# Delta-rule merges on all four 64x64 quarters of the array, with half of the diagonal blocks placed by ScalarE

## The chip, the cores and the metric

The kernel runs on one NeuronCore of a Trainium2 chip. The metric is device time in microseconds, the median of several executions. A profile is one more execution, recorded by the hardware profiler. Five engines run side by side: TensorE (PE; its weight loads are listed as PEld), VectorE (DVE), ScalarE (ACT), GpSimd (POOL) and SyncE (SP), which here only issues DMAs. Each works through its own queue in the order in which the program put the instructions there.

## The reference, cut to what matters

The layer has two branches. Branch A is a chunked gated delta rule over 8 heads and two directions, with chunks of 64 tokens. For every head and chunk the reference solves a unit lower-triangular system:

```python
a_mat = jnp.where(strict, jnp.einsum('nbhid,nbhjd->nbhij', kc * bc[..., None], kc) * decay, 0.0)
eye = jnp.eye(CHUNK, dtype=a_mat.dtype)
t_mat = lax.linalg.triangular_solve(eye + a_mat, jnp.broadcast_to(eye, a_mat.shape),
                                    left_side=True, lower=True)
```

so `t_mat` is the inverse of a 64x64 unit triangular matrix. The rest (projections with a combined `w_in`, a short convolution, the scan over chunks, differential attention in branch B, gates and the output projection) surrounds it. The sequence has 1024 latent and 256 context tokens, 1280 in all, which the kernel holds as `NT` = 10 pieces of 128 tokens; each piece has two chunks of 64. Everything is fp32; the projections split fp32 into two fp32r parts.

## The kernel before, in words

**Inverting the blocks.** `gdn_prep(h)` prepares one head. A tile `X` holds, for both directions and the 10 pieces, a 128x128 matrix. The inverse is built from blocks that double in size. The 32x32 diagonal blocks are inverted by substitution on VectorE (lines 1156 to 1161) and come back through DRAM as `R`, with `Rt` its transposed copy. Below, B(0) to B(3) are the four groups of 32 partitions, and `lo` and `hi` the two halves of 64.

Then come four groups of small matmuls, each put into TensorE's queue in one go through `mms`:

- `pz`, 32x32: 40 products, on four of the sixteen 32x32 places of the array (line 1176). VectorE writes `Z` = -pz.
- `p2` and `p3`, 32x32: 60 products on six places (line 1186). `p2` holds corner blocks for `X`; `p3` holds the corners of the 64x64 blocks for a tile `t64`, which has one 64x64 block for each of the 20 chunks. The products into `p3` share the rows of the array with a product into `p2` (B(0) or B(3)) and its columns with another one (B(1) or B(2)), in a PSUM bank of their own. ScalarE copies `p3` into `t64` (lines 1198 and 1199), and `placed` copies four blocks per chunk from `R` and `Rt` into `X` and `t64` (VectorE's line 1250 for `t64`).
- `pz6`, 64x64 (line 1212): for each of the 10 pieces one product that reads partitions `hi` and writes `lo`, and one that reads `lo` and writes `hi`. So the group uses two of the array's four 64x64 quarters, ten products each. The pieces are split over two PSUM banks: pieces 5 to 9 go into the first, pieces 0 to 4 into the second. VectorE writes `Z6` = -pz6.
- `pu6`, 64x64 (line 1222): `t64` times `Z6`, `lo` to `lo` and `hi` to `hi`: the other two quarters alone.

ScalarE copies `pu6` into `X`, scales `X` by `beta` and SyncE stores it, for the scan to load.

In the profile `pz6` and `pu6` appear as `pz` and `pu` with 64*64, since numbers at the end of a name are left out there, and `t64` as `t`. An fp32 product makes two matmul records and two weight loads, so a 64x64 group of 20 products shows 40 records.

**What sets the order.** All parts of the kernel (`gdn_prep` for each head, `placed`, the scans of both directions, the projections, the convolution) are generators that yield one step: engine, a modelled duration, what it depends on, and the function that issues the instructions. A planner (`flow`, `step`) picks the next step by modelled start times and issues it. So the order on each queue is fixed by the modelled durations, not by what happens on the chip. A step's function may issue several instructions; the planner then still counts one step on one engine.

While the heads are prepared, the projection matmuls (`mm`) fill TensorE's queue between the steps of the scan (`chain`, `out`) and of `gdn_prep`. In the scan, each piece goes from TensorE (`chain`) to ScalarE (`vd`, `vn`, lines 1323 and 1327) or VectorE (`r`, `S`) and back to TensorE.

PSUM banks for these steps come from a ring, `banks`; a step that takes a bank waits for the instructions listed with it. The bank of `p3` is listed with the two copies of lines 1198 and 1199, and a later `gram` group of the next head can be the one that takes it.

Of the kernel before, what the change touches and what calls it, by code (L numbers as in the profile page):

```python
# [23 lines left out]
NT = LT // P  # L24
# [10 lines left out]
PE, DVE, ACT, POOL, DMA, ADMA, DV2, PL1 = range(8)  # L35
# [8 lines left out]
class Block:  # L44
# [1040 lines left out]
    def gdn_prep(self, h):  # L1085
        nc, PT, V = self.nc, self.gt_, self.nc.vector
        T = lambda nm, shape, tag=None: self.g1.tile(shape, F32, tag=tag or nm, name=nm)
        G = lambda nm, shape: self.gh[h % 2].tile(shape, F32, tag=nm, name=nm)
        X = G("X", [P, 2, NT, P])
# [24 lines left out]
        for c0 in range(0, NT, 2):  # L1114
# [3 lines left out]
            for j in range(2):  # L1118
                c = c0 + j
# [20 lines left out]
        B = lambda b: slice(32 * b, 32 * b + 32)  # L1140
# [14 lines left out]
        for j in range(31):  # L1155
            n, w = 31 - j, j + 1
# [30 lines left out]
            x for c in range(NT) for x in (  # L1187
                (p2[B(0), c], R[B(0), c], Z[B(0), c]), (p2[B(1), c], Rt[B(1), NT + c], Z[B(1), c]), (p3[B(1), c], Z[B(0), c], R[B(0), c]),
                (p2[B(2), c], R[B(2), c], Z[B(2), c]), (p2[B(3), c], Rt[B(3), NT + c], Z[B(3), c]), (p3[B(2), c], Z[B(3), c], Rt[B(3), NT + c]))), 0.25
# [7 lines left out]
        self.banks.append(tx[:])  # L1197
        t6 = [(yield ACT, 0.43, [t3], lambda: nc.scalar.copy(t64[B(1), :, 0:32], p3[B(1)])),
              (yield ACT, 0.43, [t3], lambda: nc.scalar.copy(t64[B(2), :, 32:64], p3[B(2)]))]
        self.banks.append(t6[-2:])  # L1200
        yield lambda: placed
# [10 lines left out]
        t = yield PE, 1.5, [tx, b], lambda: self.mms(  # L1212
            x for cs, z in zip(halves, pz) for j in range(5) for c in (cs.start + j,) for x in (
                (z[lo, j], X[hi, 0, c, lo], X[hi, 0, c, hi]), (z[hi, j], X[lo, 1, c, hi], X[lo, 1, c, lo]))), 0.5
        tz = []
        for cs, z in zip(halves, pz):
# [23 lines left out]
    def placed(self, X, R, Rt, tt, tz, out):  # L1240
# [3 lines left out]
        tx, t6 = [], []  # L1244
# [3 lines left out]
        for (m, q, f) in ((0, slice(0, 32), R[B(0), 0:NT]), (1, slice(32, 64), R[B(1), 0:NT]), (2, slice(0, 32), Rt[B(2), NT:]),  # L1248
                          (3, slice(32, 64), Rt[B(3), NT:])):
            t6 += [(yield DV2, 0.34, [tt], lambda: V.tensor_copy(t64[B(m), :, q], f))]  # L1250
        yield lambda: tz
# [959 lines left out]
```

## Time and profile before

| | us |
|---|---|
| three runs | 1934.7, 1934.76, 1938.63 |
| their median | 1934.76 |
| the profiled execution, its own time | 1935.46 |
| its span, first to last instruction | 1933.3 |
| TensorE busy | 1896.7 (98%) |
| VectorE busy | 1453.0 (75%) |
| ScalarE busy | 1062.6 (55%) |
| GpSimd busy | 678.8 (35%) |
| first and last start of a 64x64 `pz` record | 603.9 and 1192.1 |

The span is the time from the first to the last instruction; 2.2 us of the profiled execution lie around it. Busy time of TensorE is the union of its matmuls, whose ends are modelled, so a busy share near 100% says that it had always something in flight, and not that it ran at its peak. The granted clock is full in all forty slices of the span. The merges of the eight heads lie between 595 and 1202 us, one head after the other.

### The profile page before, as it was taken

The numbers are of one execution on the slowest core, as the hardware profiler recorded it, in microseconds if no ns is written. First come the engines' busy times: TensorE is split into PE (matmuls) and PEld (weight loads), VectorE is DVE, ScalarE is ACT, GpSimd is POOL, SyncE is SP. The second block draws the span as 40 slices with busy tenths as digits, with TensorE's granted clock in tenths as the row PEclk, the third lists the DMA queues.
The fourth block names the chain that finished last, engine by engine and source line by source line (L and its number), as shares of the span: only waits on it lengthen the run. The fifth ranks groups of instructions, "written<-read, shape, count | busy, mean of one in ns | idle before, by whom it ended". The sixth has DMA issues, their size and how long they took to land.

```text
span 1933.3 us, 37454 instructions
## 1 busy us (share of the span) xinstructions
PE 1896.7 (98%) x13807; PEld 1675.3 (87%) x13807; DVE 1453.0 (75%) x3613; ACT 1062.6 (55%) x2189; POOL 678.8 (35%) x610
## 2 busy tenths in 40 slices
PE   6999999999999999999999999999999999999999
PEld 4878888899999998888888888888997888888887
DVE  4687998957887887867865865338996979995677
ACT  4543444426233563677576645439885868884222
POOL 3200000005441342343333332336766667672203
PEclk9999999999999999999999999999999999999999
DMA  9144535575545567667785565666336474226542
GB/s 335 58 137 96 138 95 138 123 190 179 165 142 183 183 191 228 216 204 232 213 292 175 195 199 150 212 231 224 132 124 210 158 238 151 93 88 213 186 157 87
DMA packets 383038, 336.39 MB, mean 174 GB/s; under 512 B 142609, under 2 KB 323443, under 8 KB 381831
## 3 DMA queue, kind: packets, MB, share of 16 engines
q1 hardware_dynamic: 382855, 333.99, 55.0%
q8 instruction: 109, 1.79, 0.4%
q14 instruction: 74, 0.61, 0.1%
HBM read 222.14 MB, written 111.79 MB: 173 GB/s over the span
## 4 chain that ended last, share of the span: by engine, by line
PE 84%; DVE 6%; DMA 4%; ACT 3%; issue 2%; SPq 1%; POOL 1%; DVEq 0%; ACTq 0%; POOLq 0%
PE mm L56 43%; PE s L56 7%; PE v L56 5%; PE chain L56 5%; PE mb L56 5%; PE ma L56 4%; PE x L56 3%; PE t L63 3%; PE out L56 3%; PE gram L56 1%; DVE S L1567 1%; DVE ac L595 1%; PE pz L56 1%; PE tr L63 1%; SPq L265 1%
## 5 line engine op out<-in xcount | busy, mean ns | idle before, releaser
L56 PE MATMUL mm<-hs,wh 128*128 128x512 f32 (+1 forms) x2048 | 648.7, 390 | 1.5 <-DVE hs L408 1.4
L56 PEld LDWEIGHTS mm<-hs,wh 128*128 128x128 f32 x2048 | 371.3, 189 | 58.7 <-DVE hs L408 2.0
L56 PE MATMUL mm<-hs,wl 128*128 128x512 f32 (+1 forms) x1024 | 397.8, 388 | 1.0 <-POOL wl L886 1.0
L56 PE MATMUL mm<-wh,hs 128*128 128x256 f32 (+1 forms) x1792 | 332.7, 286 | 0.2 <-ACT sq L978 0.2
L56 PEld LDWEIGHTS mm<-wh,hs 128*128 128x128 f32 x1792 | 281.0, 191 | 0.7 <-ACT sq L978 0.4
L1567 DVE TENSOR_SCALAR_CACHE_REDUCE S<-s,rsq 128x512 f32<-128x512 f32 (+1 forms) x384 | 239.8, 655 | 26.9 <-DMA vl<-vd 12.0
L56 PE MATMUL mm<-wl,hs 128*128 128x256 f32 (+1 forms) x896 | 256.0, 286 | 0.0
L1604 POOL TENSOR_TENSOR S<-S 128x1280 f32<-128x1280 f32 x64 | 188.9, 2955 | 92.2 <-ACT S L1597 90.9
L56 PEld LDWEIGHTS mm<-hs,wl 128*128 128x128 f32 x1024 | 194.0, 189 | 29.8 <-POOL wl L886 1.4
L1580 ACT ACTIVATE S<-S,mn 128x1280 f32<-128x1280 f32 x128 | 175.2, 1372 | 51.3 <-DVE mn L1579 50.9
L56 PEld LDWEIGHTS mm<-wl,hs 128*128 128x128 f32 x896 | 171.4, 191 | 0.1
L595 DVE SCALAR_TENSOR_TENSOR ac<-xc,convT,ac 128x1284 f32<-128x1284 f32 (+1 forms) x96 | 138.8, 1448 | 11.2 <-ACT ac L593 10.6
L56 PE MATMUL s<-kk,qh 128*128 128x512 f32 (+1 forms) x384 | 142.7, 372 | 1.9 <-DVE S L1567 1.7
L56 PE MATMUL s<-kk,ql 128*128 128x512 f32 (+1 forms) x384 | 132.9, 358 | 0.0
L1641 DVE TENSOR_TENSOR al<-t,ah 128x512 fp32r<-128x512 f32 (+1 forms) x192 | 107.0, 595 | 7.6 <-ACT ah L1636 6.3
L580 POOL MEMSET xc<- 128x2 f32 (+1 forms) x64 | 3.6, 100 | 298.5 <-ACT sq L629 113.1
L1160 DVE TENSOR_TENSOR ts<-ts,tmp 80x31 f32<-80x31 f32 (+15 forms) x248 | 94.1, 380 | 6.0
L1323 ACT ACTIVATE vd<-chain,edk 128x128 f32<-128x128 f32 x144 | 52.2, 370 | 77.8 <-PE chain L56 71.9
L56 PE MATMUL ma<-y,wh 128*128 128x512 f32 x256 | 93.0, 410 | 1.7 <-DVE g L1814 1.7
L1158 DVE TENSOR_TENSOR tmp<-ab,ts 80x31 f32<-80x31 f32 (+15 forms) x248 | 89.2, 360 | 6.6 <-DMA ab<-da 1.3
L1636 ACT CAST ah<-t 128x512 fp32r<-128x512 f32 (+1 forms) x192 | 87.9, 521 | 9.0 <-PE t L63 8.3
L56 PE MATMUL v<-al,vh 128*128 128x256 f32 x320 | 90.9, 284 | 0.7 <-DVE al L1641 0.6
(296 smaller groups left out, 4315.7 us busy)
## 6 DMA issues: line engine op xcount, KB each, us to landing
wr<-in_w_in_dram SPq DMA_DIRECT2D x48, 512.0 KB, 5.7
hx<-in_w_in_dram SPq DMA_DIRECT2D x64, 256.0 KB, 4.3
x<-xq SPq DMA_DIRECT2D x64, 256.0 KB, 5.1
X<-gcd SPq DMA_DIRECT2D x8, 1280.0 KB, 7.1
kd<-col SPq DMA_DIRECT2D x40, 256.0 KB, 2.2
xq<-X SPq DMA_DIRECT2D x16, 640.0 KB, 8.9
kk<-kd SPq DMA_DIRECT2D x16, 640.0 KB, 6.4
kq<-gkq SPq DMA_DIRECT2D x8, 1152.0 KB
```

The source lines that it names most:

```text
L56: self.nc.tensor.matmul(out, lhsT, rhs, start=start, stop=stop)
L63: self.nc.tensor.transpose(out, src, self.ident[:src.shape[0], :src.shape[0]])
L265: return DMA, us, list(deps), lambda: nc.sync.dma_start(dst, src)
L595: t = yield DV2, 1.21e-3 * wd, [t], lambda: nc.vector.scalar_tensor_tensor(ac[:, :wd], xc[:, j:j + wd], self.convw(j, x["ct"]), ac[:, :wd] ...
L1158: t = yield DV2, n * w / 960.0 + 0.08, [t if j else self.later(t, 2.5), t1], lambda: V.tensor_tensor(tv, ab[:, j + 1:, j:j + 1].to_broadca ...
L1160: t = yield DV2, n * w / 960.0 + 0.08, [t, t1], lambda: V.tensor_tensor(ts[:, j + 1:, :w], ts[:, j + 1:, :w], tv, ALU.subtract)
L1323: td = yield ACT, 0.251, [t], lambda: nc.scalar.activation(vd, pc[:, 1], AF.Copy, scale=self.edk[:, c, g:g + 1])
L1567: e = yield DVE, 0.675 if m == 512 else 0.408, [e, self.sfree[c].get(n - 4 + c)], lambda: self.nc.vector.tensor_scalar(x["S"][c][:, o:o + ...
L1580: x["x"].append((yield ACT, 1.36, [e], lambda: nc.scalar.activation(S, S, AF.Exp, bias=x["mn"][:, c:c + 1], scale=-1.0, accum_out=w["l0"][ ...
L1604: e = yield POOL, 2.9, [e], lambda: self.nc.gpsimd.tensor_tensor(S0, S0, S1, ALU.add)
L1636: e = yield ACT, 0.48 if nb == 4 else 0.27, [t, y["old", k]], lambda: self.nc.scalar.copy(y["ah", k][:, :, q], pv)
L1641: t = yield DVE, 0.603 if k < 2 else 0.322, [e, y["old", k]], lambda: self.nc.vector.tensor_tensor(y["al", k][:, :, q], pv, y["ah", k][:, ...
```

## The change

Four places change.

1. In the `p3` products, pieces 5 to 9 write the two corners to other partitions: B(3) in place of B(1), and B(0) in place of B(2).
2. The copies of `p3` into `t64` and the copies of `R`/`Rt` into `t64` are cut into pieces 0 to 4 and pieces 5 to 9. For the last five pieces the two 64x64 blocks of a piece stand in swapped halves of the partitions. The corners take four ScalarE copies of 32x5x32 in place of two of 32x10x32. Of the four VectorE copies in `placed`, each is cut to five pieces, and the same step now also issues a ScalarE copy for the other five. The planner's modelled durations and engines are as they were.
3. `pz6`: for pieces 5 to 9 the product from `hi` writes `hi` and the one from `lo` writes `lo`. The order is now piece 0, piece 5, piece 1, piece 6 and so on, so four products in a row use the four quarters.
4. `pu6`: pieces 5 to 9 read the swapped blocks of `t64` and `Z6`, so their products run from `hi` to `lo` and from `lo` to `hi`, in the same mixed order. The results stand where they stood.

```diff
         t = t3 = yield PE, 1.3, [tz, b], lambda: self.mms(
             x for c in range(NT) for x in (
...
+                (p2[B(0), c], R[B(0), c], Z[B(0), c]), (p2[B(1), c], Rt[B(1), NT + c], Z[B(1), c]),
+                (p3[B(1 if c < 5 else 3), c], Z[B(0), c], R[B(0), c]),
+                (p2[B(2), c], R[B(2), c], Z[B(2), c]), (p2[B(3), c], Rt[B(3), NT + c], Z[B(3), c]),
+                (p3[B(2 if c < 5 else 0), c], Z[B(3), c], Rt[B(3), NT + c]))), 0.25
...
-        t6 = [(yield ACT, 0.43, [t3], lambda: nc.scalar.copy(t64[B(1), :, 0:32], p3[B(1)])),
-              (yield ACT, 0.43, [t3], lambda: nc.scalar.copy(t64[B(2), :, 32:64], p3[B(2)]))]
-        self.banks.append(t6[-2:])
+        fs, ls = slice(0, 5), slice(5, 10)
+        corner = lambda m, n, q: (nc.scalar.copy(t64[B(m), fs, q:q + 32], p3[B(m), fs]), nc.scalar.copy(t64[B(n), ls, q:q + 32], p3[B(n), ls]))
+        t6 = [(yield ACT, 0.43, [t3], lambda: corner(1, 3, 0)),
+              (yield ACT, 0.43, [t3], lambda: corner(2, 0, 32))]
+        self.banks.append(t6[:])
...
         t = yield PE, 1.5, [tx, b], lambda: self.mms(
-            x for cs, z in zip(halves, pz) for j in range(5) for c in (cs.start + j,) for x in (
-                (z[lo, j], X[hi, 0, c, lo], X[hi, 0, c, hi]), (z[hi, j], X[lo, 1, c, hi], X[lo, 1, c, lo]))), 0.5
+            x for c in range(5) for f, e in ((c, lo), (c + 5, hi)) for g in (hi if e is lo else lo,) for z in (pz[f < 5],) for x in (
+                (z[e, c], X[hi, 0, f, lo], X[hi, 0, f, hi]), (z[g, c], X[lo, 1, f, hi], X[lo, 1, f, lo]))), 0.5
...
         t = yield PE, 1.5, [tz, t6, b], lambda: self.mms(
-            x for cs, u in zip(halves, pu) for j in range(5) for c in (cs.start + j,) for x in (
-                (u[lo, j], t64[lo, c], Z6[lo, c]), (u[hi, j], t64[hi, c], Z6[hi, c]))), 0.5
+            x for c in range(5) for f, e in ((c, lo), (c + 5, hi)) for g in (hi if e is lo else lo,) for u in (pu[f < 5],) for x in (
+                (u[lo, c], t64[e, f], Z6[e, f]), (u[hi, c], t64[g, f], Z6[g, f]))), 0.5
...
-            t6 += [(yield DV2, 0.34, [tt], lambda: V.tensor_copy(t64[B(m), :, q], f))]
+            t6 += [(yield DV2, 0.34, [tt], lambda: (V.tensor_copy(t64[B(m), :5, q], f[:, :5]), nc.scalar.copy(t64[B(m ^ 2), 5:, q], f[:, 5:])))]
```

The queues of GpSimd and SyncE hold the same instructions in the same order in both kernels; VectorE's differs only in the size of the copies of `placed` into `t64`. TensorE's and ScalarE's queues differ as follows.

TensorE, at the `pz6` group of head 0, before and with the change (`pz_6191` and `pz_6192` are the banks of pieces 5 to 9 and 0 to 4 before, `pz_6197` and `pz_6198` the same two with the change):

```order
 L56 MATMUL mm<-wl,hs 128x256
 L56 MATMUL mm<-wh,hs 128x256 x2
-L56 MATMUL pz_6191<-X 64x64 x10
-L56 MATMUL pz_6192<-X 64x64 x10
+L56 MATMUL pz_6198<-X 64x64 x2
+L56 MATMUL pz_6197<-X 64x64 x2
```

The two bank rows alternate five times in all with the change: still twenty products, and now in pairs that go to the two banks in turn.

ScalarE around the corner copies of head 5, before (`X<-RR` and `X<-p` place blocks in `X`, `t<-p` are the corner copies, `vd` and `vn` belong to the scan):

```order
L1247 COPY X<-RR 32x10x32 x2
L1196 COPY X<-p_11894 32x10x32
L1323 ACTIVATE vd<-chain,edk 128x128
L1327 COPY vn<-chain 128x128
L1323 ACTIVATE vd<-chain,edk 128x128
L1327 COPY vn<-chain 128x128
L1196 COPY X<-p_11894 32x10x32
L1198 COPY t_3837<-p_11895 32x10x32
L1199 COPY t_3837<-p_11895 32x10x32
```

And the same place with the change:

```order
L1251 COPY X<-RR 32x10x32 x2
L1254 COPY t_3837<-RR 32x5x32
L1198 COPY X<-p_11924 32x10x32
L1254 COPY t_3837<-RR 32x5x32 x2
L1327 ACTIVATE vd<-chain,edk 128x128
L1331 COPY vn<-chain 128x128
L1254 COPY t_3837<-RR 32x5x32
L1327 ACTIVATE vd<-chain,edk 128x128
L1331 COPY vn<-chain 128x128
L1198 COPY X<-p_11924 32x10x32
L1201 COPY t_3837<-p_11925 32x5x32 x4
```

Four new copies (`t<-RR`) stand among the scan's instructions and ahead of the corner copies, and the two corner copies have become four of half the size.

More of the change, by code (lines that the diff above doesn't have):

```diff
@@ L1187, in gdn_prep @@
             x for c in range(NT) for x in (
-                (p2[B(0), c], R[B(0), c], Z[B(0), c]), (p2[B(1), c], Rt[B(1), NT + c], Z[B(1), c]), (p3[B(1), c], Z[B(0), c], R[B(0), c]),
-                (p2[B(2), c], R[B(2), c], Z[B(2), c]), (p2[B(3), c], Rt[B(3), NT + c], Z[B(3), c]), (p3[B(2), c], Z[B(3), c], Rt[B(3), NT + c]))), 0.25
+                (p2[B(0), c], R[B(0), c], Z[B(0), c]), (p2[B(1), c], Rt[B(1), NT + c], Z[B(1), c]),
+                (p3[B(1 if c < 5 else 3), c], Z[B(0), c], R[B(0), c]),
+                (p2[B(2), c], R[B(2), c], Z[B(2), c]), (p2[B(3), c], Rt[B(3), NT + c], Z[B(3), c]),
+                (p3[B(2 if c < 5 else 0), c], Z[B(3), c], Rt[B(3), NT + c]))), 0.25
         tx, e = [], t
```

## The prediction

> **What bounds the kernel now.** I read the page's busy shares first, then the stretch in which the merges lie (590 to 1200 us), and there the chain of waits, the waits of TensorE and the timelines of single groups.
>
> From the page, the table by engine and the chain that ended last:
>
> ```profile
> PE 1896.7 (98%) x13807; PEld 1675.3 (87%) x13807; DVE 1453.0 (75%) x3613; ACT 1062.6 (55%) x2189; POOL 678.8 (35%) x610
> PE 84%; DVE 6%; DMA 4%; ACT 3%; issue 2%; SPq 1%; POOL 1%; DVEq 0%; ACTq 0%; POOLq 0%
> ```
>
> Busy time of each engine in the stretch, then the chain's shares in it and its longest links that are not TensorE's:
>
> ```profile
> 590.00:1200.00 610.00, 605.45 (x5915) 543.90 (x5914) 452.68 (x1275) 361.70 (x1002) 203.42 (x248) 1.00 0.65 206
> by line: PE mm L56 57.2%; PE chain L56 13.6%; PE out L56 7.2%; PE gram L56 3.7%; PE pz L56 2.7%; DMA hx<-tbd 1.8%; PE pu L56 1.7%; issue 1.6%; PE p L56 1.6%; DMA xq<-qk 1.4%; PE tr L63 1.2%; DMA x<-xq 1.0%; PE oT L63 0.8%; DVE fin L999 0.5%
> 624.79 10.85 DMA hx<-tbd
> 752.88 8.75 DMA xq<-qk
> 1060.31 5.95 DMA x<-xq
> ```
>
> TensorE is busy for 605 of 610 us (columns: stretch, then PE, PEld, DVE, ACT, POOL), and its groups make up nine tenths of the chain. All that it waited for there:
>
> ```profile
> PE tr L63 <- DVE fin L1000: 1.0, 1, 1.0
> PE mm L56 <- POOL wl L886: 1.0, 1, 1.0
> PE p L56 <- issue: 0.5, 1, 0.5
> PE chain L56 <- DVE S L1336: 0.5, 1, 0.5
> PE chain L56 <- DVE r L1314: 0.4, 1, 0.4
> PE chain L56 <- DMA x<-xq: 0.4, 1, 0.4
> PE chain L56 <- DVE S L1334: 0.4, 1, 0.4
> PE gram L56 <- ACT t L1199: 0.2, 1, 0.2
> ```
>
> That is 4.4 us. So TensorE's queue sets the time, and a shorter group moves what follows it; the last row also says that in one place the corner copies of `t64` hold TensorE up already.
>
> **The groups on four quarters.** One 64x64 group of head 0 and one 32x32 `pz` group in TensorE's timeline (start, duration, records):
>
> ```profile
> 603.93 1.38 PE L56 MATMUL pz<-X 64*64 64x64 f32 x40
> 605.24 0.39 PE L56 MATMUL mm<-wl,hs 128*128 128x256 f32 x1
> ...
> 595.38 0.89 PE L56 MATMUL pz<-RR,X 32*32 32x32 f32 x80
> 596.20 0.38 PE L56 MATMUL mm<-wh,hs 128*128 128x256 f32 x1
> ```
>
> From the group's first start to the next work it is 605.24 - 603.93 = 1.31 us for 40 records, 20 on each of two quarters. About 0.15 us of that is filling and draining (below, the last record of `p` starts 0.12 us ahead of the next work). So one quarter takes a record every (1.31 - 0.15) / 20 = 0.058 us. With ten records on each of four quarters a group takes 0.15 + 10 x 0.058 = 0.73 us: **0.58 us less**. Bounds: half of 1.31, 0.65, and nothing at all, if quarters that share rows or columns cannot run together.
>
> The row that comes nearest to this is the `p` group, whose products share rows (B(0) and B(3) are read twice) and columns, with different PSUM banks for the latter, just as the new order has it:
>
> ```profile
> 856.15 0.22 PE L56 MATMUL p<-Z,RR 32*32 32x32 f32 x2
> 856.16 0.21 PE L56 MATMUL p<-RR,Z 32*32 32x32 f32 x1
> 856.17 0.22 PE L56 MATMUL p<-Z,RR 32*32 32x32 f32 x2
> 856.18 0.21 PE L56 MATMUL p<-RR,Z 32*32 32x32 f32 x1
> ...
> 857.18 0.19 PE L56 MATMUL p<-RR,Z 32*32 32x32 f32 x1
> 857.30 0.50 PE L56 MATMUL mm<-hs,wh 128*128 128x512 f32 x1
> ```
>
> 120 records take 1.15 us. In the 32x32 `pz` group each place has 20 records in 0.82 us, about 0.035 us a record without filling. If a strip of rows did one product at a time, the 40 records of B(0) in `p` would need 1.4 us; they took 1.15, the whole group being paced at about 9 ns a record. So products that share rows do overlap. At 9 ns, 40 records need 0.36 us, less than 0.73, so issue doesn't bound the new groups. I take 0.58.
>
> Two rules of the Trainium skill speak against this. Its page "TensorE: Matmul & The Clock Gate", section "Part 3: Packing small matmuls — row/col tiling", says that a weight load overlaps running matmuls only where the row group differs; by that the two quarters of a row half would take turns (rival 2). The trace so far disagrees, by the 1.15 us of `p`. The same page of the skill, section "Back-to-back issue gap", states a floor of about 25 ns for small matmuls; by an estimate from it 40 records would need 1.0 us and the sum below would come to some -1 us. The trace disagrees here too, with 80 records in 0.82 us.
>
> Sixteen groups (8 heads, `pz` and `pu`): 16 x 0.58 = **9.3 us** of TensorE's time.
>
> **How much of it reaches the end.** The groups of heads 0 and 1 (four, 2.3 us) lie before or between the chain's DMA links at 624.79 and 752.88, where TensorE is not what sets the time: the transposes of `fin` already wait 1.0 us, and by the time of the second link the lead is gone. The other twelve follow, 7.0 us. The link at 1060.31 is a load of what a head stored before, so it moves with the work ahead of it. I take 0.2 us off for small waits: **6.8 us** arrive. Bounds: 9.3 if the DMA links move too, and 2.2 if the link at 1060.31 holds as well, since the eight groups of heads 2 to 5 (4.6 us) lie ahead of it.
>
> **ScalarE's added work.** Durations of copies in the stretch, by shape (count, busy us, mean ns):
>
> ```profile
> L885 ACT CAST wh<-hx 128x512 fp32r<-128x512 f32 x52 | 31.1, 616 | 5.4 <-DMA hx<-in_w_in_dram 5.1
> L1327 ACT COPY vn<-chain 128x128 f32<-128x128 f32 x103 | 27.1, 266 | 7.3 <-PE chain L56 7.3
> L1247 ACT COPY X<-RR 32x320 f32<-32x320 f32 x32 | 14.5, 454 | 1.0 <-DMA RR<-db 0.5
> L1198 ACT COPY t<-p 32x320 f32<-32x320 f32 x8 | 3.3, 417 | 0.2
> ```
>
> From SBUF, 320 columns take 454 ns and 512 take 616, so 0.84 ns a column and about 320 ns for 160. From PSUM, 128 take 266 and 320 take 417: 0.79 a column, about 291 ns for 160. A head adds four copies of 0.32 and turns two of 0.417 into four of 0.291: 1.28 + 1.16 - 0.83 = 1.61 us, and 12.9 us over eight heads. ScalarE is idle for 610 - 362 = 248 us of the stretch, mostly for TensorE:
>
> ```profile
> ACT zo L1039 <- PE mm L56: 57.1, 30, 5.3
> ACT vd L1323 <- PE chain L56: 55.9, 39, 4.2
> ```
>
> so most of the added work falls into its waits. It costs where TensorE waits for what is queued behind it: the bank of `p3`, which `gram` takes, and `vd` and `vn` of the scan. ScalarE and TensorE at head 3, and ScalarE at head 5 with TensorE's `gram` there:
>
> ```profile
> 859.13 0.42 ACT L1198 COPY t<-p 32x320 f32<-32x320 f32 x1
> 859.56 0.42 ACT L1199 COPY t<-p 32x320 f32<-32x320 f32 x1
> ...
> 860.03 0.71 PE L56 MATMUL gram<-kq 128*128 128x128 f32 x4 [0.17 <-ACT t L1199]
> ...
> 1021.47 0.42 ACT L1196 COPY X<-p 32x320 f32<-32x320 f32 x1 [0.47 <-PE p L56]
> ...
> 1022.62 0.27 ACT L1327 COPY vn<-chain 128x128 f32<-128x128 f32 x1
> 1023.79 0.42 ACT L1199 COPY t<-p 32x320 f32<-32x320 f32 x1
> ...
> 1024.63 0.38 PE L56 MATMUL gram<-kq 128*128 128x128 f32 x2
> ```
>
> At head 3 `gram` starts 0.05 us after the second corner copy, so the corners' extra 1.16 - 0.83 = 0.33 us is lost in full. At head 5 the first new copy fits into the idle 0.47 us; the other three (0.96) and the corners (0.33) push the release of the bank from 1023.79 + 0.42 = 1024.21 by 1.29 us, against 0.42 - 0.05 = 0.37 us of room before `gram`: 0.9 us lost. The other heads have one to four copies ahead of a `vd` or `vn`; I put them at 0.3 us each, one copy's length, the rest being idle time: 6 x 0.3 = 1.8. Together **3.0 us**. Bounds: the two places that the rows show, 1.2, and all of 12.9.
>
> **VectorE.** Its four copies a head are cut in half:
>
> ```profile
> L1250 DVE COPY t<-RR x32: 307/318/814, 602.9 to 1190.2; 32x320 f32<-32x320 f32 x32
> ```
>
> At most 4 x 0.16 = 0.64 us a head. VectorE is idle for 157 us of the stretch and these copies are followed by the substitution of a later head; I count nothing, and up to 1 us as a bound. The `p3` products only change place: 0. The evacuations of `pz6` and `pu6` find both banks complete at the end of the group, where before one was ready halfway; that end is now as early as the old half: 0.
>
> **The sum.** -6.8 + 3.0 - 0.2 (VectorE) = -4.0 us. From the profiled execution's own 1935.46 (span 1933.3 and 2.2 around it) that gives 1931.5; it lies 0.7 above the median of 1934.76, so the median should come to **1930.8**.
>
> **Rivals.**
>
> 1. *ScalarE's copies are hidden and the DMA links move with TensorE.* For it: 248 us of idle ScalarE. Against it: the two `gram` places. Between -5.5 and -9.3; at its end 1925.5.
> 2. *Quarters that share rows take turns.* The groups gain nothing and ScalarE's 3.0 us stay: 1937.8. Against it: the `p` group.
> 3. *Quarters that share PSUM partitions half overlap*, since two products then write the same partitions at once. A group gains half, 0.29 us, 16 x 0.29 = 4.6, of which by the same share (6.8 of 9.3) 3.4 arrive; with +3.0 and -0.2 about 1934.2. Against it: B(1) and B(2) in `p`, which two products write.
> 4. *Slower: ScalarE becomes what the scan waits for.* The planner does not count the new copies, so they stand among `vd` and `vn`, and each may delay the recurrence that two directions share. If all 12.9 us reach TensorE, the sum is +6.1: 1940.9. It decides from the point where more than 10.7 us of the 12.9 (6.8 + 3.9) are exposed. For it: the order at head 5. Against it: 113 us in which `zo` and `vd` wait for TensorE.
>
> **How the numbers follow.** Chances: the forecast 0.64, rival 1 0.15, rival 2 0.08, rival 3 0.05, rival 4 0.08. A difference of 0.2% is 3.9 us, about what a measurement of this kernel can tell from none, and the forecast sits on that edge: somewhat over half of its chance (0.35) lies beyond it. Faster: 0.35 + 0.15 = 0.50. Within 0.2%: 0.29 of the forecast, 0.05 of rival 3, and 0.06 of rival 2, whose +3.0 stays mostly under the edge: 0.40. Slower: 0.02 of rival 2 and 0.08 of rival 4: 0.10. The range takes in most of rival 1 and a part of rival 2: 1926.5 to 1936.5.
>
> **What the profile of the changed kernel would show.** Right: 64x64 groups that last about 0.73 us from first start to the next work, ScalarE busy about 13 us more, VectorE 2 to 4 us less, TensorE's waits for `gram` and `chain` behind ScalarE 2 to 3 us longer, and a lead at TensorE that grows between 760 and 1200 us and is constant after. Wrong in the first term: groups still at 1.3 us (rival 2) or at 1.0 (rival 3). Wrong in the second: a lead of 9 us at 1200, or one lost at a DMA link. Wrong in the third: TensorE's waits for ScalarE near zero, or above 10 us.

## The result and the profile after

| | before | with the change |
|---|---|---|
| median of the runs, us | 1936.36 (22 runs) | 1933.22 (22 runs) |
| lowest to highest | 1932.28 to 1938.63 | 1930.07 to 1937.47 |
| ratio to before, 95% interval | | 0.9986 (0.998 to 0.9992) |
| profiled execution, its span | 1935.46, 1933.3 | 1933.29, 1931.2 |

The change is **2.7 us faster** by the ratio (1936.36 x 0.0014; by the interval 1.5 to 3.9). That is a gain that the runs can tell from nothing, but it lies within 0.2%. The forecast was -4.0 us, 1930.8. Of the 2.4 us by which 1933.22 misses it, 1.6 come from the first three runs of before, whose median of 1934.76 was low, and the rest from the sum (the two medians lie 3.1 us apart, the ratio says 2.7). The prediction gave 0.50 to a gain beyond 0.2% and 0.40 to one within it; it was the second.

The page of the changed kernel, its table by engine; then, by engine, the stretch in which the merges lie (columns as in the prediction):

```profile
PE 1890.5 (98%) x13807; PEld 1665.9 (86%) x13807; DVE 1450.8 (75%) x3613; ACT 1075.3 (56%) x2237; POOL 678.1 (35%) x610
```

```profile
590.00:1200.00 610.00, 600.94 (x5920) 535.98 (x5919) 451.73 (x1278) 375.74 (x1057) 202.69 (x248) 1.00 0.65 206
```

ScalarE has 14.0 us more in the stretch (361.70 before), VectorE only 0.95 less, TensorE 4.5 less. The span fell by 2.1 only. TensorE's waits in the stretch, the longer ones (what waited, for what: us in total, times, longest):

```profile
PE tr L63 <- DVE fin L1000: 1.2, 1, 1.2
...
PE gram L56 <- ACT t L1201: 1.0, 2, 0.5
PE pu L56 <- DVE Z L1221: 0.9, 1, 0.9
PE chain L56 <- DVE S L1340: 0.8, 2, 0.5
...
PE chain L56 <- DMA sk<-gkq: 0.6, 1, 0.6
PE chain L56 <- DMA vv<-gv: 0.5, 1, 0.5
PE chain L56 <- DVE r L1318: 0.5, 1, 0.5
PE tr L63 <- DVE Z L1221: 0.4, 1, 0.4
...
PE chain L56 <- ACT vn L1331: 0.4, 1, 0.4
```

All rows together add up to 8.5 us, against 4.4 before. New are the waits for `Z` (VectorE), for `vn` (ScalarE) and for `sk` and `vv` (loads of the scan); the wait for the corner copies (`t`, ScalarE) grew from 0.2 to 1.0.

**The groups** became as short as predicted. The two 64x64 groups of head 0 in TensorE's timeline:

```profile
603.19 0.81 PE L56 MATMUL pz<-X 64*64 64x64 f32 x40
603.93 0.39 PE L56 MATMUL mm<-wl,hs 128*128 128x256 f32 x1
...
606.74 0.81 PE L56 MATMUL pu<-Z,t 64*64 64x64 f32 x40 [0.88 <-DVE Z L1221]
607.48 0.38 PE L56 MATMUL mm<-wh,hs 128*128 128x256 f32 x1
```

603.93 - 603.19 = 0.74 us, where before it was 1.31. In three of the sixteen groups (heads 1, 6 and 7) a gap inside the group makes it 0.07 to 0.5 us longer. But `pu` waits 0.88 us for `Z`, which takes back more than `pz` had saved.

**The copies**, by shape, in the stretch (count, busy us, mean ns):

```profile
L1254 ACT COPY t<-RR 32x160 f32<-32x160 f32 x32 | 10.3, 323 | 0.6
L1254 DVE COPY t<-RR 32x160 f32<-32x160 f32 x32 | 9.9, 310 | 0.6
L1201 ACT COPY t<-p 32x160 f32<-32x160 f32 x32 | 9.1, 283 | 0.5
```

ScalarE's copies last 323 and 283 ns (320 and 291 predicted). VectorE's copies of half the size take 310 ns; the whole ones had a median of 318.

**Where the 9.1 us went.** Every TensorE instruction of the one trace can be set beside the same one of the other, and the difference of their starts followed from 590 us (-0.88, a difference that the start of the program left) to 1250 (-2.9). From one instruction to the next it moves by:

| TensorE's instructions | us |
|---|---|
| inside the sixteen 64x64 groups | -8.8 |
| waits for VectorE's `Z` and `fin`, heads 0 and 1 (at 607, 640, 687 and 702 us of before) | +1.9 |
| waits for VectorE's `r` and `S` (783, 1090, 1095) | +1.4 |
| waits for ScalarE: `gram` at heads 3 and 5 (860, 1024), `vd`/`vn` (953, 1024) | +1.8 |
| waits for the scan's loads `vv` and `sk` (864, 925) | +1.5 |
| gaps in front of `p` and `pz` or inside them | +1.0 |
| waits of before that fell away (`chain`, `p`) | -2.5 |
| steps under 0.12 us each, mostly at `chain` | +1.7 |

The sum is -2.0, and each row is good to some tenths. This is one pair of profiled executions. How much two executions part by themselves shows at 590 us, where the order of work has hardly begun to differ: the traces of this document stand there between -2.0 and +0.5 us against the trace of before. So only what moves within a short stretch is read from such a pair, and the runs of the experiments below say how far it holds.

The two places that the prediction picked for ScalarE. ScalarE and TensorE at head 3, then at head 5:

```profile
857.34 1.17 ACT L1201 COPY t<-p 32x160 f32<-32x160 f32 x4
...
858.55 0.71 PE L56 MATMUL gram<-kq 128*128 128x128 f32 x4 [0.50 <-ACT t L1201]
...
1024.01 1.17 ACT L1201 COPY t<-p 32x160 f32<-32x160 f32 x4
...
1025.23 0.49 PE L56 MATMUL gram<-kq 128*128 128x128 f32 x2 [0.46 <-ACT t L1201]
```

At both, `gram` starts right behind the corner copies. The difference of starts grows there by 0.32 us (0.33 predicted) and by 0.30 + 0.63 = 0.93, the wait of `chain` for `vd` included (0.9 predicted).

VectorE at head 0 shows the loss that was not predicted:

```profile
603.96 0.32 DVE L1254 COPY t<-RR 32x160 f32<-32x160 f32 x1
604.30 0.30 DVE L1160 TENSOR_TENSOR ts<-ts,tmp 80x135 f32<-80x135 f32 x1
604.63 0.32 DVE L1158 TENSOR_TENSOR tmp<-ab,ts 80x156 f32<-80x156 f32 x1
604.98 0.32 DVE L1160 TENSOR_TENSOR ts<-ts,tmp 80x156 f32<-80x156 f32 x1
605.34 0.34 DVE L1158 TENSOR_TENSOR tmp<-ab,ts 80x175 f32<-80x175 f32 x1
605.71 0.89 DVE L1221 TENSOR_SCALAR Z<-pz 128x320 f32<-128x320 f32 x2
```

`pz` is complete at 604.0, but VectorE has the substitution of the next head (`tmp`, `ts`) and a copy in its queue ahead of `Z`, one right behind the other, and comes to `Z` at 605.71. Before, in the same queue:

```profile
606.47 0.89 DVE L1217 TENSOR_SCALAR Z<-pz 128x320 f32<-128x320 f32 x2
```

There `pz` ended at 605.2 and `Z` came 1.2 us later; with the change `pz` ends 1.2 us sooner, `Z` comes only 0.76 sooner and so 1.7 us behind it. From the first record of `pz` to the first of `pu` it took 3.18 us before and 3.55 now: the group is 0.57 shorter, and the time until `pu` longer. In heads 1 to 3 this distance grew too, by 0.1 to 0.25 us; in heads 4 to 6 it became 0.5 to 0.6 shorter, and in head 7 0.1.

### The profile page after: what moved, and what is told of

Read it like the earlier page. It is cut to its first block, busy times and chain, and to the rows that moved or that the text cites. A ratio compares the mean times of both kernels' runs of the same rounds, so it can differ in the third digit from the quotient of the medians.

```text
span 1931.2 us, 37500 instructions
## 1 busy us (share of the span) xinstructions
PE 1890.5 (98%) x13807; PEld 1665.9 (86%) x13807; DVE 1450.8 (75%) x3613; ACT 1075.3 (56%) x2237; POOL 678.1 (35%) x610
## 4 chain that ended last, share of the span: by engine, by line
PE 82%; DVE 7%; DMA 4%; ACT 4%; issue 2%; POOL 1%; SPq 1%; ACTq 0%; DVEq 0%; POOLq 0%
PE mm L56 42%; PE s L56 7%; PE v L56 6%; PE chain L56 5%; PE mb L56 5%; PE ma L56 4%; PE x L56 3%; PE t L63 3%; PE out L56 3%; PE gram L56 1%; DVE S L1571 1%; DVE ac L595 1%; PE tr L63 1%; PE mp L56 1%; DMA hx<-tbd 1%
## 5 line engine op out<-in xcount | busy, mean ns | idle before, releaser
L595 DVE SCALAR_TENSOR_TENSOR ac<-xc,convT,ac 128x1284 f32<-128x1284 f32 (+1 forms) x96 | 138.8, 1449 | 12.9 <-ACT ac L593 12.2
```

The costliest lines, as they stand in the source:

```text
L595: t = yield DV2, 1.21e-3 * wd, [t], lambda: nc.vector.scalar_tensor_tensor(ac[:, :wd], xc[:, j:j + wd], self.convw(j, x["ct"]), ac[:, :wd] ...
```

## The experiments

The prediction's terms were: 9.3 us of TensorE's time, of which 6.8 arrive, and +3.0 for ScalarE. The runs give only their sum, -2.7. Two theories stand on either side of these terms. **A**: little of TensorE's time reaches the end, and ScalarE's copies cost next to nothing. **B**: nearly all of it reaches the end, and ScalarE's copies eat most of it. All ratios are to the kernel before on the same chip, and us are what that ratio is away from 1, times its median. An interval of 0.2% is 3.9 us wide, so most of these numbers are known to about 2 us either way.

| what runs | ratio (95%) | us against before |
|---|---|---|
| the change | 0.9986 (0.998, 0.9992) | -2.7 |
| before, each group twice | 1.0095 (1.0082, 1.0109) | +18.4 |
| the change, pieces in order | 1.0006 (0.9997, 1.0015) | +1.2 |
| the change, ScalarE's half copies on VectorE | 1.0006 (0.9997, 1.0015) | +1.2 |
| the change, VectorE's half copies on GpSimd | 0.998 (0.997, 0.999) | -3.9 |
| the change, ScalarE's half copies on GpSimd | 0.9971 (0.996, 0.9981) | -5.6 |
| the change, both halves on GpSimd | 0.9969 (0.9959, 0.9979) | -6.0 |
| four quarters, VectorE turns back | 0.9983 (0.9974, 0.9992) | -3.3 |
| four quarters, ScalarE turns back | 0.9979 (0.997, 0.9989) | -4.1 |
| VectorE turns back, copies on GpSimd | 0.9981 (0.9971, 0.9991) | -3.7 |
| before, copies on GpSimd | 1.0001 (0.9992, 1.001) | +0.2 |
| ScalarE turns back, copies on GpSimd | 0.9965 (0.9952, 0.9978) | -6.8 |
| the same on another chip | 0.9957 (0.9945, 0.997) | -8.3 |

### Does TensorE's time reach the end?

**Each group twice**, in the kernel before:

```diff
-            x for cs, z in zip(halves, pz) for j in range(5) for c in (cs.start + j,) for x in (
+            x for _ in range(2) for cs, z in zip(halves, pz) for j in range(5) for c in (cs.start + j,) for x in (
```

and the same for `pu6`.

> The kernel before with every 64x64 group issued twice (the second writes the same values again): TensorE has 16 x 1.17 = 18.7 us more in the same places. Theory of the prediction (TensorE's queue sets the time but for the waits at a few DMA links): +14 to +18.7 us (ratio 1.007 to 1.0097). Rival A (a third of TensorE's time in these places reaches the end): +6 (1.003). Rival B: +18 to +18.7 (1.0095).

It came out 18.4 us slower. TensorE's timeline at head 0:

```profile
604.49 2.55 PE L56 MATMUL pz<-X 64*64 64x64 f32 x80
606.97 0.39 PE L56 MATMUL mm<-wl,hs 128*128 128x256 f32 x1
```

A group lasts 606.97 - 604.49 = 2.48 us where one lasted 1.31, so 16 x 1.17 = 18.7 us were added, and 98% of them arrive (by the interval 85% and more). Theory A in its simple form falls: these groups do set the time. But added and saved time are not the same thing, as the next runs show.

**The change with the pieces in order**: the same products into the same quarters, the same copies, but pieces 0 to 4 first and 5 to 9 behind them, as before:

```diff
-            x for c in range(5) for f, e in ((c, lo), (c + 5, hi)) for g in (hi if e is lo else lo,) for z in (pz[f < 5],) for x in (
+            x for f, c, e in [(j, j, lo) for j in range(5)] + [(j + 5, j, hi) for j in range(5)] for g in (hi if e is lo else lo,) for z in (pz[f < 5],) for x in (
```

and the same for `pu6`.

> The change, but pz6 and pu6 issue pieces 0 to 4 first and then 5 to 9, so that only two quarters work at a time; all copies stay as in the change. Theory of the prediction: the groups last 1.3 us again and ScalarE's 3.0 us stay alone: +2.5 to +3 us against the kernel before (ratio 1.0014). Rival A: 0 (1.0000). Rival B: +6 (1.0031). If the groups still last 0.74 us, the order of issue is not what brings the overlap.

It came out at +1.2 us. TensorE's timeline:

```profile
603.66 1.21 PE L56 MATMUL pz<-X 64*64 64x64 f32 x40
604.80 0.39 PE L56 MATMUL mm<-wl,hs 128*128 128x256 f32 x1
```

The groups last 1.14 us and not 1.31, since the second five pieces begin in their own two quarters while the first are still running: in the trace the records start two by two every 0.058 us, and from 0.40 us on four by four for three such steps. So this run has groups 0.40 us longer than the change, 6.4 us in all, and is 3.9 us slower: about 61% of TensorE's time arrives at the end. The intervals of the two runs leave this share between about a third and nine tenths: less than all, but no sharper. If the same share holds for the 0.57 us of the change, 0.61 x 9.1 = 5.5 us of its saving arrive, and 5.5 - 2.7 = 2.8 us is what the copies cost. In this run itself 0.61 x 16 x 0.17 = 1.7 arrive, so that 1.2 + 1.7 = 2.9 is the cost of the copies: the same number by the same step, not a second proof.

### Which engine takes the rest?

**ScalarE's half copies given to VectorE**:

```diff
-            t6 += [(yield DV2, 0.34, [tt], lambda: (V.tensor_copy(t64[B(m), :5, q], f[:, :5]), nc.scalar.copy(t64[B(m ^ 2), 5:, q], f[:, 5:])))]
+            t6 += [(yield DV2, 0.34, [tt], lambda: (V.tensor_copy(t64[B(m), :5, q], f[:, :5]), V.tensor_copy(t64[B(m ^ 2), 5:, q], f[:, 5:])))]
```

> The change with the ScalarE copies of placed given back to VectorE, as two copies of 32x5x32 in place of one of 32x10x32; the four corner copies stay on ScalarE. Theory of the prediction (TensorE's 9.1 us arrive as 6.8, ScalarE's added work costs 3.0): of the 3.0 only the corners' part of some 1 us stays, VectorE gets 2 us more work a head, mostly in its idle time, so about -5 us against the kernel before (ratio 0.9974). Rival A (ScalarE's copies cost nothing, only a third of TensorE's saving arrives): -2.7, as the change itself (0.9986). Rival B (nearly all of TensorE's saving arrives, and ScalarE's copies cost 6): -8 (0.9959).

It came out at +1.2 us, on the wrong side of each of these: the run does not take ScalarE's cost away, it moves it to an engine that is closer to the bound. Copies by shape, then the stretch and TensorE's two longest waits in it:

```profile
L1254 DVE COPY t<-RR 32x160 f32<-32x160 f32 x64 | 19.8, 310 | 1.1
```

```profile
590.00:1200.00 610.00, 597.17 (x5899) 532.51 (x5898) 461.02 (x1304) 362.34 (x1008) 202.61 (x248) 1.00 0.65 206
```

```profile
PE pu L56 <- DVE Z L1221: 2.3, 1, 2.3
PE chain L56 <- DVE S L1340: 1.6, 4, 0.7
```

A head has eight copies of 310 ns on VectorE in place of four: 9.9 us more than in the change, and the end is 3.9 us later, although ScalarE was relieved by as many copies. Against the run below in which the same copies are on GpSimd it is 1.2 + 5.6 = 6.8 us later, about seven tenths of what VectorE got. VectorE is busy for 461 of 610 us, 76%, and yet most of what is added to it here arrives.

The next three take the copies away from the two engines instead, to GpSimd, which was busy for 203 us of the stretch. **VectorE's half to GpSimd:**

```diff
-            t6 += [(yield DV2, 0.34, [tt], lambda: (V.tensor_copy(t64[B(m), :5, q], f[:, :5]), nc.scalar.copy(t64[B(m ^ 2), 5:, q], f[:, 5:])))]
+            t6 += [(yield DV2, 0.34, [tt], lambda: (nc.gpsimd.tensor_copy(t64[B(m), :5, q], f[:, :5]), nc.scalar.copy(t64[B(m ^ 2), 5:, q], f[:, 5:])))]
```

> The change, with the 32 half copies of diagonal blocks that it leaves on VectorE (32 x 0.31 = 9.9 us) given to GpSimd; ScalarE keeps all that the change gave it. Theory V: what eats TensorE's saving is VectorE's order of work, in which the Z that the next group waits for stands behind other operations; then taking 9.9 us away from VectorE brings the change from -2.7 to about -5.5 us against the kernel before. Theory S: what eats it is ScalarE's added 14 us alone; then this stays at -2.7 (within 1 us). A third outcome, slower than the change, would mean that GpSimd's copies come too late for the solve.

**ScalarE's half to GpSimd:**

```diff
-            t6 += [(yield DV2, 0.34, [tt], lambda: (V.tensor_copy(t64[B(m), :5, q], f[:, :5]), nc.scalar.copy(t64[B(m ^ 2), 5:, q], f[:, 5:])))]
+            t6 += [(yield DV2, 0.34, [tt], lambda: (V.tensor_copy(t64[B(m), :5, q], f[:, :5]), nc.gpsimd.tensor_copy(t64[B(m ^ 2), 5:, q], f[:, 5:])))]
```

> The change, with ScalarE's 32 half copies of diagonal blocks (32 x 0.323 = 10.3 us, L1254) given to GpSimd instead; VectorE keeps its halves. Theory S: -5.5 us against the kernel before. Theory V: -2.7 to -3.5, since VectorE has as much to do as in the change. If both this and the other half's move give about -5.5, each engine is a bound of its own at different places.

**Both halves to GpSimd**, both edits together:

> The change, with both halves of the diagonal copies on GpSimd: VectorE loses 9.9 us and ScalarE 10.3. Theories V and S together (each engine limits at its own places): -7 us against the kernel before, as the version that turns Z back on ScalarE with these copies on GpSimd gave (-6.8). If VectorE alone limits, the same as with VectorE's half moved alone. If GpSimd becomes late with 64 copies, nearer -2.7.

(The version with -6.8 us that this expectation names is shown in the next part.) They gave -3.9, -5.6 and -6.0 us. So ScalarE's 10.3 us of copies cost 5.6 - 2.7 = 2.9 us, theory S's number; VectorE's 9.9 us cost 1.2 with ScalarE's copies in place, a difference that the intervals don't separate from zero, and 0.4 without them. (Of the 9.9 us only 4.5 show up as less busy time, 447.22 against 451.73 in the stretch; the last section comes back to this.) (The intervals of the change and of ScalarE's half on GpSimd just touch, at 0.998 and 0.9981, so 2.9 is known to about two microseconds either way.) Neither theory had the third run right: with both engines relieved it is -6.0 and not -7, hardly more than with ScalarE alone.

The traces say where. The start of the same TensorE instruction against the trace of before, ahead of head 0's two groups, behind them, and behind head 1's:

| | at 597 us | at 610 | at 750 |
|---|---|---|---|
| the change | -0.87 | -0.94 | -0.47 |
| ScalarE's half on GpSimd | -0.51 | -0.56 | -0.51 |
| VectorE's half on GpSimd | +0.47 | -0.19 | -0.94 |
| both halves on GpSimd | -1.29 | -2.25 | -2.75 |
| ScalarE's half on VectorE | +0.21 | +1.95 | +3.0 |

Head 0's two groups save 1.1 us. There it is VectorE alone that decides: with its copies gone 0.7 and 1.0 us of it stay, with its copies in place 0.1, whether ScalarE's are gone or not, and with eight copies on it 1.7 us are lost. What follows up to 750 us is not as clean. In the run with VectorE's half on GpSimd 1.2 us more come at 640 us, where TensorE waits for `fin`, a VectorE product that is slow in the trace of before and not in this one (the last section shows it), and head 1 keeps nothing of its groups. With both halves on GpSimd, 0.8 us of the lead go at 762 us, where TensorE waits 1.3 us for `r` and VectorE ahead of that for the load `xq`, the second of the prediction's DMA links. More is lost behind 860 us, where both directions' scans begin to use what was loaded for them. With VectorE's half on GpSimd, the longest wait of TensorE; then a row of its timeline with ScalarE's half on GpSimd (a second such wait there takes 2.1 us):

```profile
PE chain L56 <- DMA sk<-gkq: 1.8, 1, 1.8
```

```profile
868.37 0.68 PE L56 MATMUL chain<-S,sk 128*128 128x128 f32 x4 [2.28 <-DMA sk<-gkq]
```

In the trace of before no such wait exists. In the view of the DMA issues between 850 and 960 us, the load of `sk`, 640 KB, lands 8.1 us after its issue before, 9.6 with the change and 10.5 with ScalarE's half on GpSimd (the last number of a row, here of a single landing):

```profile
sk<-gkq SPq DMA_DIRECT2D x2, 640.0 KB, 8.1
```

```profile
sk<-gkq SPq DMA_DIRECT2D x2, 640.0 KB, 9.6
```

```profile
sk<-gkq SPq DMA_DIRECT2D x2, 640.0 KB, 10.5
```

TensorE waits for `vv` and `sk` for 1.1 us in the change and for 0.7 to 4.4 us in the runs with copies on GpSimd (of each one profiled execution). Being ahead makes such a wait possible: before, the load of 8.1 us landed 0.4 us ahead of its use. But it doesn't make the load slow: with the pieces in order, and in all versions of the next part, the same view has 7.6 to 8.4 us, also where TensorE is 3 us ahead. Why the load takes 9.2 to 10.5 us in the change and in the four runs that give its half copies to another engine is open.

### Other ways to use four quarters

Here the blocks of `t64` stay where they were, `p3` and its copies as before, and only the results are turned back: `Z6` of pieces 5 to 9 is written with its two halves swapped, and `pu6` of these pieces comes out in swapped halves, which ScalarE's two existing copies put right. **VectorE turns back** (against the change):

```diff
+                (p2[B(0), c], R[B(0), c], Z[B(0), c]), (p2[B(1), c], Rt[B(1), NT + c], Z[B(1), c]), (p3[B(1), c], Z[B(0), c], R[B(0), c]),
...
+        t6 = [(yield ACT, 0.43, [t3], lambda: nc.scalar.copy(t64[B(1), :, 0:32], p3[B(1)])),
...
+            tz += [(yield DVE, 0.398, [t], lambda: V.tensor_scalar_mul(Z6[:, cs], z, -1.0) if cs.start == 0 else (
+                V.tensor_scalar_mul(Z6[lo, cs], z[hi], -1.0), V.tensor_scalar_mul(Z6[hi, cs], z[lo], -1.0)))]
...
+                (u[e, c], t64[lo, f], Z6[lo, f]), (u[g, c], t64[hi, f], Z6[hi, f]))), 0.5
...
+            f = [(yield ACT, 0.43, [t], lambda: nc.scalar.copy(X[lo, 0, cs, hi], u[lo if cs.start == 0 else hi])),
...
+            t6 += [(yield DV2, 0.34, [tt], lambda: V.tensor_copy(t64[B(m), :, q], f))]
```

> Four quarters without new copies: t64 and the corners as before; pz6 as in the change; VectorE turns the swapped halves of pieces 5 to 9 back when it writes Z6 (two 64-partition instructions in place of one of 128, 0.48 us more a head), pu6 of pieces 5 to 9 reads lo and writes hi and the other way round, and ScalarE's copies out of pu6 turn them back. ScalarE has no instruction more than before. Theory of the prediction: TensorE's part alone, less some waits for Z6: -6 us against the kernel before (ratio 0.9969). Rival A: -2.7 (0.9986). Rival B: -8 to -9 (0.9956).

It gave -3.3 us: one instruction more a head on VectorE and none on ScalarE, in place of six more on ScalarE, came out about the same as the change. From here on two theories stand against each other. **C**: TensorE's lead is lost where VectorE's queue has no gap between `pz6` and `pu6`. **D**: it is lost at DMA links, whatever VectorE does. Then **ScalarE turns back** those two halves:

```diff
-                V.tensor_scalar_mul(Z6[lo, cs], z[hi], -1.0), V.tensor_scalar_mul(Z6[hi, cs], z[lo], -1.0)))]
+                nc.scalar.mul(Z6[lo, cs], z[hi], -1.0), nc.scalar.mul(Z6[hi, cs], z[lo], -1.0)))]
```

> As the kernel that turns the halves back, but ScalarE instead of VectorE writes Z6 of pieces 5 to 9, with two copies of 64x320 (0.42 us each) that turn the halves and change the sign. VectorE has one instruction of 0.48 us less a head than before, ScalarE 0.84 us more. Theory C: half of Z6 no longer waits in VectorE's queue, but the other half still does; -4 to -5 us against the kernel before (ratio 0.9977). Theory D: -3, less what ScalarE's 6.7 us cost, so -2 (0.999).

It gave -4.1 us, inside what theory C said, but its interval (-5.8 to -2.1) all but reaches theory D's -2 and takes in the -3.3 of VectorE turning back. Then **the four diagonal copies a head on GpSimd**, with VectorE turning back:

```diff
-            t6 += [(yield DV2, 0.34, [tt], lambda: V.tensor_copy(t64[B(m), :, q], f))]
+            t6 += [(yield DV2, 0.34, [tt], lambda: nc.gpsimd.tensor_copy(t64[B(m), :, q], f))]
```

> As the kernel that turns the halves back (four quarters, no copy more on ScalarE, 0.48 us a head more on VectorE), with the four copies of 32x10x32 a head from R and Rt into t64 moved from VectorE to GpSimd, at the same places of the program. VectorE loses 4 x 0.32 us a head and GpSimd, which is busy for 203 of 610 us, gets them. Theory C (TensorE's lead is lost where VectorE's queue has no gap between pz6 and pu6): the lead survives in more heads, -6 to -8 us against the kernel before (ratio 0.9964). Theory D (VectorE's queue does not matter; the lead is lost at DMA links): -3.3 as without the move (0.9983). If GpSimd's copies are slow and late, worse than -3.3.

It gave -3.7 us, nearer to theory D's number. The same edit in the **kernel before**:

> The kernel before with the four copies a head into t64 moved from VectorE to GpSimd, nothing else. Theory C: VectorE holds TensorE up in places before the change too, so about -2 us against the kernel before (ratio 0.999). Theory D: 0.

It gave +0.2 us: nothing. VectorE is busy for 5 us less there (447.55 in the stretch, 452.68 without the edit), and nothing waits for it long enough to gain by it. And **both**, ScalarE turning back and the copies on GpSimd:

> Both moves at once: ScalarE writes Z6 of pieces 5 to 9, GpSimd copies R and Rt into t64. VectorE has 1.76 us less a head than before (8 x 1.76 = 14 us). Theory C: -7 to -9 us against the kernel before (ratio 0.9959). Theory D: -2 (0.999).

> The version with Z's second half turned back by ScalarE and the four diagonal copies a head on GpSimd, once more beside the three others on one chip: -6.8 us again if its first six runs stand (0.9965); within 0.2% of the kernel before if they were a chance of that chip.

They gave -6.8 us, and -8.3 on another chip: 0.35 to 0.43% faster than before, the best here, and faster than the change by the intervals of both. That is theory C's number for the two edits together. Against VectorE turning back they were worth 0.8 and 0.4 us singly, which the intervals don't separate from nothing, and 3.5 and 5.0 together; that they give more together than the sum is likely, but with about 2 us of doubt on each number it isn't certain. VectorE at head 0, and TensorE there:

```profile
604.31 0.49 DVE L1217 TENSOR_SCALAR Z<-pz 128x320 f32<-128x320 f32 x1
...
602.91 0.81 PE L56 MATMUL pz<-X 64*64 64x64 f32 x40
...
605.52 0.81 PE L56 MATMUL pu<-Z,t 64*64 64x64 f32 x40
```

`Z` starts 0.7 us after `pz` ended (1.7 with the change), ScalarE writes the other half meanwhile, and `pu` follows `mm` without a wait, 2.61 us after `pz` began and not 3.55. In all of the stretch TensorE does not wait for `Z` in this trace (for 0.2 us in the one from the other chip); among its longest waits are now:

```profile
PE chain L56 <- DMA vv<-gv: 1.2, 1, 1.2
...
PE tr L63 <- DVE fin L1000: 1.0, 2, 0.5
PE chain L56 <- DMA sk<-gkq: 0.9, 1, 0.9
```

## Why the prediction was right or wrong

**The group's length: right.** 0.74 us against 0.73 predicted, and 16 x 0.57 = 9.1 us against 9.3. Products that share rows of the array, and products that share its columns with their own banks, ran side by side, as `p` had shown. Rivals 2 and 3 fall by this row.

The two rules of the Trainium skill that spoke against the change, both on its page "TensorE: Matmul & The Clock Gate", don't hold here. By "Part 3: Packing small matmuls — row/col tiling" a weight load overlaps running matmuls only where the row group differs, so that the two quarters of a row half would take turns. By an estimate from the floor of about 25 ns in the same page's "Back-to-back issue gap" 40 records would need 1.0 us. The trace disagrees with both: 40 records, a product of each row half and column half in turn, started within 0.59 us and the group was done after 0.74.

**ScalarE's +3.0: right in its size and at the two places that were worked out.** These showed 0.32 and 0.93 us (0.33 and 0.9 predicted). The run without ScalarE's half copies gives 2.9 in all, and the step by way of the pieces in order 2.8, both to about 2 us. The other 1.8, 0.3 us a head for six heads, was a guess that the trace does not bear out: the profiled pair shows 1.8 us for all waits that can be seen, so 0.5 outside the two places, and the rest is not found as waits. That the total fits is in this part luck. Rival 4, in which 10.7 us or more of the 12.9 are exposed, is far off. The argument held at the two places because it asked what is queued behind the copies at each place, and not how long ScalarE is idle.

**How much arrives: 6.8 predicted, about 5.5 by the runs.** This is the step that failed, in its reasons more than in its amount. Two ways give the amount: the pieces in order (0.61 x 9.1 = 5.5), and the change without ScalarE's half copies, which gave -5.6, or about -6 if the corners' four copies for two cost some tenths there. The 1.3 us are the difference between -4.0 and -2.7, but 5.5 is known only to about 2 us, so the runs don't tell it from 6.8. The reasons were these:

- The loss at heads 0 and 1 was there (2.3 us predicted; at 750 us nothing of them was left), but it was put to DMA links that would hold TensorE whatever it did. The load `hx` of the first link is issued at 624.79 us before and at 623.85 with the change, as far ahead as TensorE is, so that link moves. At the second, `xq`, the change loses nothing either; it gains 0.7 us at 762 us, where before TensorE waited for what this load feeds. Only versions with a larger lead lose some there (0.8 us with both halves on GpSimd), so this part of the argument is not all wrong. What held TensorE at head 0 was VectorE's queue, in which `Z` stood behind the substitution of the next head: all five traces with the diagonal copies off VectorE keep 0.7 to 1.0 of that head's 1.1 us, and the five in mixed order that leave copies on it keep 0.1 or lose. The prediction read VectorE's idle 157 us over the whole stretch and did not look at the 3 us in which `Z` was due.
- For the twelve later groups it took off 0.2 us for "small waits". The pair of traces shows 1.4 us for `r` and `S` and 1.5 for `vv` and `sk`, against 2.5 that fell away, and 1.7 in steps too small to name. So the lead did not grow steadily from 760 to 1200 us, as it was to do: it was gone at 960 us (+0.1) and came back later. A lead lost at loads was one of the prediction's own signs of being wrong in this term.

**VectorE's -0.2 and its halved copies: the premise was wrong.** The sum has 0.2 us that the prediction's own paragraph counts as nothing. A halved copy takes as long as a whole one to within 3% (medians of 309 and 318 ns). The copies together still fell from 12.5 to 9.9 us, since the whole copies that took up to 814 ns are gone, but VectorE's busy time fell by 0.95 us in the stretch, not by 2 to 4. The price was small, since the term was small. But it hid that the change, which was to share the copies between two engines, left VectorE's queue about as long as it was and lengthened ScalarE's.

**Rival 1** (-5.5 to -9.3, all hidden) did not come true for the change. The versions that take the added copies off ScalarE reach -5.6 and -6.0, and the one that turns back on ScalarE with the copies on GpSimd -6.8 and -8.3: that is what four quarters are worth in this kernel when little else stands in the way (there VectorE has less to do than before, which without four quarters gains nothing: +0.2).

**What stays open.** Why the load of `sk` takes 9.2 us and more in some of the runs and about 8 in others was not taken apart. Nor was how the difference between -6.8 and -8.3 of one and the same kernel is divided between chips and chance; its two intervals overlap.

## What to carry to other kernels

- On an engine that is busy 98% of the time, time added counts in full (98% here), but time taken away counts only down to the next engine's queue: about 61% here (a third to nine tenths by the intervals). So before a saving is counted, look in the timeline of every engine that hands results to the shortened group at what stands ahead of that result in its queue, within the few microseconds in which it would now be due; the engine's busy share (75%) says nothing on that.
- A copy that is cut in half to be shared between engines can cost twice: the half can stay as long as the whole on the one (309 and 318 ns here), and the other gets new work. Relief of one place may show nothing that can be measured until a second is relieved as well (0.8 and 0.4 us alone, 3.5 and more together), so try such edits together too.

## What the hardware showed that was not expected

**Half of a copy took VectorE as long as the whole.** The copy of 32x160 with the change, and that of 32x320 before (least, median, longest ns) from the view of one line:

```profile
L1254 DVE COPY t<-RR x32: 297/309/317, 602.1 to 1189.2; 32x160 f32<-32x160 f32 x32
```

```profile
L1250 DVE COPY t<-RR x32: 307/318/814, 602.9 to 1190.2; 32x320 f32<-32x320 f32 x32
```

Half the columns save 9 ns of 318 at the median. Width alone is not the reason, since another operation of VectorE on 160 columns is much shorter in the trace of before:

```profile
L835 DVE TENSOR_SCALAR gtmp<-gtmp 128x160 f32<-128x160 f32 x8 | 1.9, 240 | 0.2
```

The halved copies also have five pieces, an odd number, in place of ten, and no run here separates the two. (The mean of the wide ones is higher, 391 ns, by seven that took 467 to 814 ns. All seven lie beside an instruction of GpSimd; eleven of the narrow ones do too, and none is longer than 317 ns.) On ScalarE the same step from 320 to 160 columns saved 131 of 454 ns, and on GpSimd 139 of 477:

```profile
L1250 POOL COPY t<-RR 32x320 f32<-32x320 f32 x32 | 15.3, 477 | 1.1
```

```profile
L1254 POOL COPY t<-RR 32x160 f32<-32x160 f32 x32 | 10.8, 338 | 1.1
```

(GpSimd's rows are of the kernel before with the copies on GpSimd, and of the change with VectorE's half there.)

**In these traces VectorE's work is slow only beside GpSimd's.** In the stretch of before, take the shapes of VectorE instructions that occur at least five times with no GpSimd instruction running. Of 814 instructions alone none took over 1.2 times its shape's median; of 410 beside a GpSimd instruction 46 did. One of them is the `fin` that TensorE waits for at 640 us, as long as the GpSimd product beside it, where the median of its shape is 0.42 us:

```profile
637.14 2.63 DVE L999 TENSOR_TENSOR fin<-raw,hx 128x256 f32<-128x256 f32 x1
...
637.05 2.44 POOL L886 TENSOR_TENSOR wl<-wr,wh 128x1024 fp32r<-128x1024 f32 x1 [2.51 <-ACT wh L885]
```

So work given to GpSimd can come back as time of VectorE. With VectorE's half copies on GpSimd, VectorE has 9.9 us of copies less in the stretch but is busy only 4.5 less. Two groups of the substitution and of `placed` by shape, with the change and then with those copies on GpSimd:

```profile
L1250 DVE COPY X<-RR 32x320 f32<-32x320 f32 x32 | 13.7, 429 | 0.8
...
L1158 DVE TENSOR_TENSOR tmp<-ab,ts 80x60 f32<-80x60 f32 x14 | 3.0, 214 | 0.3
```

```profile
L1250 DVE COPY X<-RR 32x320 f32<-32x320 f32 x32 | 14.9, 467 | 0.8
...
L1158 DVE TENSOR_TENSOR tmp<-ab,ts 80x60 f32<-80x60 f32 x14 | 5.9, 420 | 0.3
```

The same products of 80x60 take 214 ns (mean) in the one and 420 in the other, and the copies into `X` go from 429 to 467. Which instruction is hit is a matter of when the two engines meet, and other products of the substitution became shorter.

**Quarters overlap even where the code does not mix them.** With the pieces in order the two pairs of quarters came one after the other in the queue, and the group still lasted 1.14 us instead of 1.31.
